# Prompt attention in a hybrid decoder layer: the products with V of a piece as one run behind all of its transposes

## The chip, the cores and the metric

The kernel runs on one core of a Trainium2 chip. A core has a matrix engine, TensorE (PE in the profile; PEld is its weight load, which overlaps the matmuls), and three engines that work on tiles: VectorE (DVE), ScalarE (ACT) and GpSimd (POOL). SyncE (SP) issues this kernel's DMAs, which a set of 16 DMA engines carries out. TensorE reads from the on-chip memory SBUF and writes into the banks of PSUM, from where DVE or ACT fetch the result.

The metric is the time of one execution on the device, in microseconds (us); the median of several runs counts, and less is better. A profiled execution gives the durations of single instructions.

## The reference

One inference step of a decoder layer, for one prompt of 1024 tokens and 8 x 8 sample tokens. Cut to what matters here:

```python
def dilated_group_prompt(q, k, v, window, dilation):      # (128,1), (512,4), (2048,16)
    ...
    s = jnp.einsum('brnqhd,brnkhd->brnhqk', qs, kk) * SCALE
    ...
    s = jnp.where(mask[None, None, :, None], s, NEG_INF)
    o, lse = softmax_attend(s, vv, 'brnhqk,brnkhd->brnhqd')
...
def trunk_layer(x, ...):
    h = rms_norm(x, norm_mix_g)
    proj = h @ w_in
    ...                                  # split into a_val, a_gate, q, k, v
    a = jax.nn.silu(layer_norm(depthwise_conv_valid(a_full, conv_a_w, conv_a_b), ln_a_g, ln_a_b))
    o = attend(q, k, v).reshape(B, S, D_ATTN)
    x = x + jnp.concatenate([a, o], axis=-1) @ w_out
    h = rms_norm(x, norm_ffn_g)
    g = depthwise_conv_valid(g_full, ffn_conv_w, ffn_conv_b)
    x = x + (jax.nn.silu(g) * (h @ w_ffn_up)) @ w_ffn_down
```

There are 12 heads of 64 columns. Each query sees its neighbours at three strides, and the three partial softmaxes are merged, which is the same as one softmax over all the (query, key) pairs with a count for pairs that occur more than once.

## The kernel before

**Stages.** The 1088 tokens (1024 of the prompt, 64 of the samples) lie along the free axis. First come the projections into Q, K and V, one pair of heads (128 columns) after another, six pairs in all; the products of a projection are three for each weight (high and low parts, lines 183 to 185 in `gemm`), accumulated in PSUM tiles `g`. Q, K and V are written to DRAM (`dq`, `dk`, `dv`) and read back per head by `load_head`. Attention of the prompt begins while pair 3 is projected and is spread between the projections of pairs 3 to 5; the rest lies in a stage of its own beside the attention of the samples and the output projection (`out_part`, whose products are also lines 183 to 185 and whose sums into `x` are line 858). The last part of the output projection (lines 960 to 974, products 911 to 914, sums 1061) opens the next stage, and then the feed-forward network follows.

**A piece.** Prompt attention of one head is cut into two pieces of 512 queries (`u` 0 and 1), 24 pieces in all. `scores` (line 650) multiplies Q and K into PSUM `s`, once for the near window ("near", in blocks of neighbouring tokens, Q tile `qw`) and once for the strided neighbours ("far", Q tile `qs`); DVE adds the masks (L654). `exchange` (L628) shares the maxima. Then `weighted` does, for the piece before:

1. the exponentials on ACT (L691), in place, into the weights `y`, queries on the partitions;
2. for each of three (`u` = 0) or four (`u` = 1) **groups** of weights: three or four transposes on TensorE (L718) into one of two PSUM banks `t`; a copy of that bank into an SBUF tile `ph` of the tag "H", by ACT (L724), or for one group by DVE (L722); then the products with V (L735) that use it, V being the stationary operand (64 columns), into the single bank `o`: near ones with `vw` into partitions 0 to 63, far ones with `vf` into 64 to 127;
3. ACT copies one half of `o` out (`ot`, L738) and DVE adds the other (`un`, L739).

`normalise` follows after a pair of heads: `db` (L748), four transposes (L751), the quotient `cat` (L753) and its DMA into `mixed` in DRAM (L755). `load_mixed` (L267 to L270) reads `mixed` back for the output projection and splits it into the parts `mh` and `ml`; L960 to L963 do so for the last part.

**What sets the order.** The program is written in one order; a scheduler with a simulated timeline gives each engine its own order from it, taking among what is ready what has the highest priority, which is by default what was written first. `tc.issue_after(x)` keeps an instruction behind `x` on its engine. Each engine then works through its list strictly in order: an instruction that has to wait holds up everything behind it on that engine. Products with V wait for a place in the list like everything else, so rows of the projections, of `scores` and of other transposes stand between them.

**Buffers.** `KB, VB, QB, YB, HB, UB, PT = 4, 2, 2, 7, 5, 2, 2` in line 51: V has two tiles (`vf`, loaded at L607, and `vw`, loaded at L610 in four DMAs), which is one pair of heads, so the next pair's V can be loaded only after the last product with V of the pair before. Q has two tiles (`qs` by L595 and `qw`, made from it by POOL at L597), one head. H has five tiles, used by `ph`, `ot`, `db` and `cat`; there is one bank `o` and there are two banks `t`. Weight tiles of the output projection (`wr`, L153) have two buffers, and SP issues all DMAs in one list.

Of the kernel before, what the change touches and what calls it, by code (L numbers as in the profile page):

```python
# [24 lines left out]
P = 128  # L25
# [22 lines left out]
NCH = NCACHE // CH  # L48

TB, WB, ZA, GA = 5, 5, 4, 2  # L50
KB, VB, QB, YB, HB, UB, PT = 4, 2, 2, 7, 5, 2, 2
DCOPY = ((2,), (2,))
SBUFS = {"S": (3, 3, 2), "U": (3, 3, 1)}
NS1, PN = 3, 4
HEADS = (0, 5, 8)
# [24 lines left out]
def trunk_kernel(tc, xT, w_in, w_out, w_gate, w_up, w_down, par, kc, vc, sa, sf, pmask, smask,  # L80
                 yT, kT, vT, ca, cas, cf):
    nc = tc.nc
    with (
# [31 lines left out]
        def bank(z, tag, bufs):  # L115
            return zone[z + "ps"].tile([P, 512], F32, tag=tag, name=nm(tag), bufs=bufs)

        def zt(z, tag, bufs, s, w=N, dt=F32):
            return zone[z].tile([P, w], dt, tag=tag, name=nm(s), bufs=bufs)
# [44 lines left out]
        def load_cache(Z, src):  # L164

            t = zt(Z, "C", SBUFS[Z][0], "cr", 4 * CH)
            cached.append(nc.sync.dma_start(t, src).ins)
# [345 lines left out]
        def sample_attention(p, Z, masks):  # L513
            mask, z = masks
            SB, PB = SBUFS[Z][1:]
            _, new, vn = spill[p]
# [166 lines left out]
        def weighted(p, hd, u, sc, den, un):  # L683

            near, far, m = sc
            vf, vw = [v[:, :, hd * 64:hd * 64 + 64] for v in values[p]]
            r0 = slice(hd * 64, hd * 64 + 64)
            r1 = slice(64 - hd * 64, 128 - hd * 64)
            for g, ys in ((0, near), (1, far)):
                for i, y in enumerate(ys):  # L690
                    nc.scalar.activation(y, y, AF.Exp, bias=m[:, 4 * g + i:4 * g + i + 1], scale=-1.0,  # L691
                                         accum_out=den[:, g, 2 * hd + u, i:i + 1])
            po = bank("P", "o", 1)
            pw = po.rearrange("p (c i j) -> p c i j", c=4, j=32)


            near_jobs, far_jobs = [], []
            for kb in range(max(4 * u - 1, 0), 4 * u + 4):
                qs = [i for i in (kb - 4 * u, kb + 1 - 4 * u) if 0 <= i < 4]
                ts = [near[i][:, -P:] if kb == 4 * u + i else near[i][:, :P] for i in qs]  # L700
                near_jobs.append((0, ts, vw[:, kb], pw[:64, :, qs[0]:qs[-1] + 1, :]))
            for c in range(4):
                for k in range(u + 1):
                    far_jobs.append((1, [far[c][:, k * P:k * P + P]], vf[:, 2 * c + k], po[64:, c * P:c * P + P]))

            n, f = near_jobs, far_jobs
            if u == 0:
                group = [[n[0], f[0], f[1]], [n[2], f[2], f[3]], [n[1], n[3]]]
            else:
                group = [[n[1], f[0], f[1]], [n[3], f[2], f[3]], [n[2], f[4], f[5]], [n[0], f[6], n[4], f[7]]]  # L710
            done = [[], []]
            left = [len(n), len(f)]
            for gi, jobs in enumerate(group):
                pt = bank("P", "t", PT)
                o = 0
                for _, ts, _, _ in jobs:
                    for t in ts:
                        nc.tensor.transpose(pt[:, o:o + P], t, ident)  # L718
                        o += P
                th = zt("P", "H", HB, "ph", 512)  # L720
                if gi in DCOPY[u]:
                    nc.vector.tensor_copy(th[:, :o], pt[:, :o])  # L722
                else:
                    nc.scalar.activation(th[:, :o], pt[:, :o], AF.Copy)  # L724
                o = 0
                for x, ts, v, dst in jobs:
                    left[x] -= 1
                    w = P * len(ts)
                    m = th[:, o:o + w]
                    if x == 0:  # L730
                        m = m.rearrange("p (s c j) -> p c s j", c=4, j=32)
                    with ExitStack() as order:
                        for b in (done[x][:1] if x else done[x][:2]):
                            order.enter_context(tc.issue_after(b))
                        done[x].append(nc.tensor.matmul(dst, v, m, start=not done[x], stop=(left[x] == 0)).ins)  # L735
                    o += w
            ot = zt("P", "H", HB, "ot", 512)
            nc.scalar.activation(ot[r0, :], po[r1, :], AF.Copy)  # L738
            nc.vector.tensor_add(un[u][r0, :], po[r0, :], ot[r0, :])  # L739
# [39 lines left out]
        def finish():  # L779
            for b in before:  # L780
                weighted(*b)
                if b[1:3] == (1, 1):
                    normalise(b[0], *b[4:])
            before.clear()
# [47 lines left out]
        first = [0]  # L832
# [121 lines left out]
        n = PARTS[-1]  # L954
# [368 lines left out]
        raws, moving, lows, done = {}, [], [], []  # L1323
# [60 lines left out]
        w, act = [], []  # L1384
# [45 lines left out]
        for k, (g, unit) in enumerate(UNITS):  # L1430
# [16 lines left out]
            for i, product in enumerate(unit):  # L1447
                b, key, outs = product
                for m in range(4):
# [6 lines left out]
                    for r, h in outs:  # L1456
                        x = x2[4 * r + m][:, h * HN:h * HN + HN]
# [176 lines left out]
```

## Time and profile before

| | |
|---|---|
| time, median of 3 runs | 1351.49 us (1349.26 to 1357.11) |
| the profiled execution: its time | 1352.69 us |
| the profiled execution: span of its records | 1350.9 us, mean granted TensorE clock 0.992 |
| TensorE busy in the span | 1313.0 us (97%) |
| DVE, ACT, POOL busy | 945.5 us (70%), 558.2 us (41%), 474.1 us (35%) |
| first and last product with V (L735) | 260.7 us and 568.4 us |

The span is the stretch from the first record to the last; the execution's own time is 1.8 us more. Times in rows count from the start of the span. A row of the timeline has the start, the duration, the engine, the line, the operation, the tile written and the tiles read, the shape, and how many such instructions are put together (x4); in brackets stands how long the engine was idle before it, and what released it. Matmuls overlap in TensorE: of two rows that follow each other without a gap, it is the distance of their starts that counts, not the duration. "PEclk" in a row of a window is the clock that TensorE was granted there, as a share of full speed.

### The profile page before, as it was taken

What the parts mean: (1) busy time and instruction counts of PE and PEld (TensorE: products, weight loads), DVE (VectorE), ACT (ScalarE), POOL (GpSimd) and SP (SyncE); (2) the same over time, 40 slices, a digit from 0 to 9 for tenths busy, and PEclk for the clock granted to TensorE, in tenths of its full rate; (3) what the DMA queues carried; (4) which work ended last, traced back from release to release, by engine and by line L of the source; (5) the groups of instructions that cost most, each with busy time, mean ns of one, the idle gap of its engine ahead of it and who ended that gap; (6) DMA issues with size and microseconds to landing.
All of it is one profiled execution on the core that took longest, in us unless ns stands there. A gap on an engine that the chain in (4) does not pass through costs nothing.

```text
span 1350.9 us, 25872 instructions
## 1 busy us (share of the span) xinstructions
PE 1313.0 (97%) x10275; PEld 1247.8 (92%) x10275; DVE 945.5 (70%) x1789; ACT 558.2 (41%) x1128; POOL 474.1 (35%) x375
## 2 busy tenths in 40 slices
PE   7999999999999999999999999999999999999996
PEld 7999988998977787898999999999999999999996
DVE  6378779556675556768987776677766669967656
ACT  6312111456574466335553333333333335334432
POOL 1321112111111100731475465554655534444710
PEclk9999999999999999999999999999999999999998
DMA  8247684935689786453033322332213296352412
GB/s 287 60 142 278 227 287 173 242 112 144 179 271 268 214 264 206 160 202 110 1 121 106 106 67 86 121 107 104 81 73 121 73 335 233 107 171 98 154 40 95
DMA packets 92762, 210.28 MB, mean 156 GB/s; under 512 B 13792, under 2 KB 42720, under 8 KB 92640
## 3 DMA queue, kind: packets, MB, share of 16 engines
q1 hardware_dynamic: 92640, 208.62, 47.4%
q8 instruction: 81, 1.33, 0.4%
q14 instruction: 41, 0.34, 0.1%
HBM read 152.55 MB, written 56.04 MB: 154 GB/s over the span
## 4 chain that ended last, share of the span: by engine, by line
PE 82%; DVE 8%; DMA 6%; issue 2%; ACT 1%; SPq 1%; DVEq 0%; ACTq 0%
PE g L183 6%; PE g L185 6%; PE g L184 6%; PE py L913 4%; PE py L911 4%; PE py L914 4%; PE g L911 4%; PE g L913 4%; PE g L914 4%; PE o L735 3%; PE pz L911 3%; PE pz L913 3%; PE pz L914 3%; PE px L911 3%; PE px L914 3%; PE px L913 3%
## 5 line engine op out<-in xcount | busy, mean ns | idle before, releaser
L159 POOL TENSOR_TENSOR wl<-wr,wh 128x1024 fp32r<-128x1024 f32 (+1 forms) x36 | 66.8, 1855 | 350.5 <-PE g L185 274.1
L183 PE MATMUL g<-xh,wh 128*128 128x384 f32 (+1 forms) x472 | 157.8, 334 | 0.6 <-DVE qkv L446 0.6
L184 PE MATMUL g<-xl,wh 128*128 128x384 f32 (+1 forms) x472 | 156.6, 332 | 0.0
L185 PE MATMUL g<-xh,wl 128*128 128x384 f32 (+1 forms) x472 | 156.4, 332 | 0.0
L911 PE MATMUL g<-ux,as 128*128 128x272 f32 x504 | 145.1, 288 | 1.0 <-DVE x L1458 0.9
L914 PE MATMUL g<-ux,as 128*128 128x272 f32 x504 | 145.3, 288 | 0.0
L913 PE MATMUL g<-ux,as 128*128 128x272 f32 x504 | 144.7, 287 | 0.0
L1016 POOL TENSOR_TENSOR wb<-wr,wb 128x512 fp32r<-128x512 f32 x84 | 120.9, 1449 | 57.3 <-ACT wb L1015 57.3
L1368 POOL TENSOR_TENSOR as<-ar,as 128x640 fp32r<-128x640 f32 (+1 forms) x56 | 91.3, 1640 | 102.7 <-ACT as L1367 89.9
L1015 ACT ACTIVATE wb<-wr 128x512 fp32r<-128x512 f32 x84 | 52.4, 627 | 154.4 <-DVE wr L1032 94.5
L1016 POOL TENSOR_TENSOR wa<-wr,wa 128x512 fp32r<-128x512 f32 x42 | 65.1, 1553 | 138.4 <-ACT wa L1015 117.3
L691 ACT ACTIVATE y<-y,m 128x128 f32<-128x128 f32 (+1 forms) x192 | 88.4, 463 | 20.0 <-DVE m L679 20.0
L911 PEld LDWEIGHTS g<-ux,as 128*128 128x128 f32 x504 | 95.0, 189 | 1.3 <-ACT as L1367 1.1
L914 PEld LDWEIGHTS g<-ux,as 128*128 128x128 f32 x504 | 94.8, 188 | 0.0
L913 PEld LDWEIGHTS g<-ux,as 128*128 128x128 f32 x504 | 94.7, 188 | 0.0
L654 DVE CUSTOM_DVE_ANT_0 y<-s,pmk 128x128 f32<-128x128 f32 (+1 forms) x192 | 64.1, 378 | 41.7 <-PE s L650 31.7
L1238 DVE SCALAR_TENSOR_TENSOR fc<-gb,prm,fc 128x1104 f32<-128x1104 f32 x44 | 82.5, 1894 | 14.9 <-ACT fc L1236 14.4
L183 PEld LDWEIGHTS g<-xh,wh 128*128 128x128 f32 x472 | 89.0, 189 | 3.1 <-issue 1.8
L185 PEld LDWEIGHTS g<-xh,wl 128*128 128x128 f32 x472 | 89.0, 189 | 2.3 <-issue 2.1
L184 PEld LDWEIGHTS g<-xl,wh 128*128 128x128 f32 x472 | 89.2, 189 | 0.6 <-issue 0.2
L396 DVE SCALAR_TENSOR_TENSOR cacc<-gp,prm,cacc 128x1024 f32<-128x1024 f32 x60 | 86.6, 1443 | 0.0
L157 ACT ACTIVATE wh<-wr 128x1024 fp32r<-128x1024 f32 (+1 forms) x36 | 29.6, 822 | 111.6 <-PE g L185 79.5
(370 smaller groups left out, 4288.7 us busy)
## 6 DMA issues: line engine op xcount, KB each, us to landing
cr<-in_kc SPq DMA_DIRECT2D x24, 768.0 KB, 6.9
cr<-in_vc SPq DMA_DIRECT2D x24, 768.0 KB, 7.3
ux<-ub SPq DMA_DIRECT2D x63, 272.0 KB, 4.3
kk<-dk SPq DMA_DIRECT2D x48, 256.0 KB, 6.1
wr<-in_w_gate SPq DMA_DIRECT2D x22, 512.0 KB, 3.3
wr<-in_w_up SPq DMA_DIRECT2D x22, 512.0 KB, 4.3
wr<-in_w_in SPq DMA_DIRECT2D x20, 512.0 KB, 5.7
ub<-u SPq DMA_DIRECT2D x18, 544.0 KB, 4.4
```

What stands on the lines that cost most here:

```text
L159: lo_eng.tensor_sub(lo, raw, hi.bitcast(F32))
L183: nc.tensor.matmul(ps[c], whi[:, k, :], xh[:, t0:t0 + n], start=(k == 0), stop=False)
L184: nc.tensor.matmul(ps[c], whi[:, k, :], xl[:, t0:t0 + n], start=False, stop=False)
L185: nc.tensor.matmul(ps[c], wlo[:, k, :], xh[:, t0:t0 + n], start=False, stop=(k == nk - 1))
L396: eng.scalar_tensor_tensor(acc[:, :S], gp[:, j:j + S], col(w0 + j), acc[:, :S], op0=ALU.mult, op1=ALU.add)
L691: nc.scalar.activation(y, y, AF.Exp, bias=m[:, 4 * g + i:4 * g + i + 1], scale=-1.0, accum_out=den[:, g, 2 * hd + u, i:i + 1])
L911: nc.tensor.matmul(ps, whi[:, k, :], xh[:, t], start=(start and k == 0), stop=False, skip_group_check=True)
L913: nc.tensor.matmul(ps, whi[:, k, :], xl[:, t], start=False, stop=False, skip_group_check=True)
L914: nc.tensor.matmul(ps, wlo[:, k, :], xh[:, t], start=False, stop=(k == nk - 1), skip_group_check=True)
L1016: nc.gpsimd.tensor_sub(lo, x, hi.bitcast(F32))
L1238: nc.vector.scalar_tensor_tensor(c[:, :W], gb[i][:, t:t + W], col(C_FW + 3 * f + t), c[:, :W], op0=ALU.mult, op1=ALU.add)
L1368: nc.gpsimd.tensor_sub(lo, raw, hi.bitcast(F32))
```

## The change

H gets 8 tiles in the place of 5. `weighted` takes the groups in another order (group 0 last), and for each only transposes and copies; the tiles are kept in `turned`. Then all products with V of the piece follow, each kept directly behind the one before by `tc.issue_after`, the group that was copied last first, and with a priority raised by 4000 places of the written order.

```diff
-KB, VB, QB, YB, HB, UB, PT = 4, 2, 2, 7, 5, 2, 2
+KB, VB, QB, YB, HB, UB, PT = 4, 2, 2, 7, 8, 2, 2
 DCOPY = ((2,), (2,))
+AHEAD = 4000
...
-            done = [[], []]
-            left = [len(n), len(f)]
-            for gi, jobs in enumerate(group):
+            turned = []
+            for gi in (*range(1, len(group)), 0):
+                jobs = group[gi]
                 pt = bank("P", "t", PT)
                 o = 0
                 for _, ts, _, _ in jobs:
...
                     nc.scalar.activation(th[:, :o], pt[:, :o], AF.Copy)
-                o = 0
-                for x, ts, v, dst in jobs:
-                    left[x] -= 1
-                    w = P * len(ts)
-                    m = th[:, o:o + w]
-                    if x == 0:
-                        m = m.rearrange("p (s c j) -> p c s j", c=4, j=32)
-                    with ExitStack() as order:
-                        for b in (done[x][:1] if x else done[x][:2]):
-                            order.enter_context(tc.issue_after(b))
-                        done[x].append(nc.tensor.matmul(dst, v, m, start=not done[x], stop=(left[x] == 0)).ins)
-                    o += w
+                turned.append((jobs, th))
+            done = []
+            left = [len(n), len(f)]
+            with tc.high_priority(offset=AHEAD):
+                for jobs, th in turned[-1:] + turned[:-1]:
+                    o = 0
+                    for x, ts, v, dst in jobs:
+                        w = P * len(ts)
+                        m = th[:, o:o + w]
+                        if x == 0:
+                            m = m.rearrange("p (s c j) -> p c s j", c=4, j=32)
+                        first = left[x] == len((n, f)[x])
+                        left[x] -= 1
+                        with tc.issue_after(done[-1]) if done else nullcontext():
+                            done.append(nc.tensor.matmul(dst, v, m, start=first, stop=(left[x] == 0)).ins)
+                        o += w
```

The number of products, transposes, copies and DMAs is the same. Below, products with V are L735 before and L740 with the change; other lines behind the edit go up by one to five (L183 becomes L184, L718 L719, L724 L725, L738 L743, L650 L651, L269 L270).

**On TensorE, in the first piece** (bank `o_2433`, during a projection, whose products are those into `g`): two of the three groups before, with transposes between them.

```order
L735 MATMUL o_2433<-ph_2439,vw_2321 64x4x64
L735 MATMUL o_2433<-ph_2439,vf_2319 64x128 x2
L718 MATMUL t_2454<-ident,y_2342 128x128
L718 MATMUL t_2454<-ident,y_2350 128x128
L735 MATMUL o_2433<-ph_2449,vw_2321 64x4x64
L735 MATMUL o_2433<-ph_2449,vf_2319 64x128 x2
L718 MATMUL t_2454<-ident,y_2350 128x128
```

The third group stands 24 rows further on, behind products of the projection. With the change, the same place reads:

```order
L184 MATMUL g_3454<-xh_132,wh_3325 128x384
L740 MATMUL o_2433<-ph_2452,vw_2321 64x4x64
L740 MATMUL o_2433<-ph_2452,vf_2319 64x128 x2
L740 MATMUL o_2433<-ph_2439,vw_2321 64x4x64
L740 MATMUL o_2433<-ph_2439,vf_2319 64x128 x2
L740 MATMUL o_2433<-ph_2445,vw_2321 64x4x64
L740 MATMUL o_2433<-ph_2445,vw_2321 64x4x32
L651 MATMUL s_2480<-kk_2374,qw_2372 128x128
```

All products of the piece now stand in one run, from the last group copied to the others, between products of the projection and those of `scores`. Over the whole program there are 67 such runs before and 24, one for each piece, with the change, and TensorE's list changes 234 times before and 160 times with the change between rows that write 128 partitions, 64 and 32.

**On ACT, at the end of the last projection** (the piece whose products go into `o_3843`, pair 2, second head): `ph` are copies of transposed weights, `ot` the copy out of `o`, `y` the exponentials of the next piece, and `mh` the high parts for the output projection. Before:

```order
L738 ACTIVATE ot_3787<-o_3745 64x512
L724 ACTIVATE ph_3849<-t_3844 128x512
L724 ACTIVATE ph_3859<-t_3854 128x512
L691 ACTIVATE y_3808,den_3092<-y_3808,m_3832 128x256 x2
L691 ACTIVATE y_3816,den_3092<-y_3816,m_3832 128x256 x2
L691 ACTIVATE y_3792,den_3092<-y_3792,m_3832 128x256 x2
L691 ACTIVATE y_3800,den_3092<-y_3800,m_3832 128x256 x2
L738 ACTIVATE ot_3872<-o_3843 64x512
L724 ACTIVATE ph_3946<-t_3941 128x512
L724 ACTIVATE ph_3956<-t_3951 128x512
L269 ACTIVATE mh_4619<-mx_4617 128x1088
```

With the change:

```order
L743 ACTIVATE ot_3787<-o_3745 64x512
L270 ACTIVATE mh_4619<-mx_4617 128x1088
L725 ACTIVATE ph_3849<-t_3844 128x512
L270 ACTIVATE mh_4625<-mx_4623 128x1088
L725 ACTIVATE ph_3862<-t_3857 128x512
L270 ACTIVATE mh_4631<-mx_4629 128x1088
L743 ACTIVATE ot_3872<-o_3843 64x512
```

The splits `mh`, which wait for DMAs, stood behind the copies and the `ot` of this piece and now stand between them; the run of products that needs these copies has one small product (a row of `exchange`) between itself and its last transposes on TensorE.

**On TensorE, in the last piece** (`o_5871`, during the output projection): before, its last two groups.

```order
L735 MATMUL o_5871<-ph_5897,vw_5052 64x4x64
L735 MATMUL o_5871<-ph_5897,vf_5050 64x128 x2
L185 MATMUL g_6432<-mh_6282,wl_6416 128x384
L735 MATMUL o_5871<-ph_5907,vw_5052 64x4x32
L735 MATMUL o_5871<-ph_5907,vf_5050 64x128
L735 MATMUL o_5871<-ph_5907,vw_5052 64x4x32
L735 MATMUL o_5871<-ph_5907,vf_5050 64x128
L183 MATMUL g_6443<-mh_6270,wh_6414 128x320
```

With the change:

```order
L186 MATMUL g_6516<-mh_6282,wl_6500 128x384
L740 MATMUL o_5871<-ph_5898,vw_5052 64x4x64
L740 MATMUL o_5871<-ph_5898,vf_5050 64x128 x2
L740 MATMUL o_5871<-ph_5877,vw_5052 64x4x64
L740 MATMUL o_5871<-ph_5877,vf_5050 64x128 x2
L740 MATMUL o_5871<-ph_5884,vw_5052 64x4x64
L740 MATMUL o_5871<-ph_5884,vf_5050 64x128 x2
L740 MATMUL o_5871<-ph_5891,vw_5052 64x4x32
L740 MATMUL o_5871<-ph_5891,vf_5050 64x128
L740 MATMUL o_5871<-ph_5891,vw_5052 64x4x32
L740 MATMUL o_5871<-ph_5891,vf_5050 64x128
L184 MATMUL g_6527<-mh_6270,wh_6498 128x320
```

The run stands later among the rows of the output projection: 119 rows of this stage follow the last product with V before, and 65 with the change. On SP, the last write of `cat` and the reads of `mixed` behind it now come without the last loads of weights between them.

## The prediction

> **What bounds the kernel now.** I read the whole first (shares by engine), then windows over the stretch in which prompt attention runs (255 to 575 us), then TensorE's waits there, and then single places on the timeline. The chain of work that ended last, by engine:
>
> ```profile
> PE 82%; DVE 8%; DMA 6%; issue 2%; ACT 1%; SPq 1%; DVEq 0%; ACTq 0%
> ```
>
> The windows give for each stretch its length, then the busy time of TensorE, of its weight loads, DVE, ACT and POOL with instruction counts, the granted clock, the DMA share and GB/s.
>
> ```profile
> 255.00:300.00 45.00, 45.00 (x320) 40.98 (x318) 25.53 (x99) 25.12 (x79) 6.88 (x4) 1.00 0.56 161
> 300.00:375.00 75.00, 74.47 (x556) 69.02 (x556) 47.61 (x164) 45.95 (x126) 9.93 (x6) 1.00 0.59 164
> 375.00:425.00 50.00, 46.13 (x361) 38.05 (x360) 35.18 (x148) 31.41 (x100) 5.45 (x6) 1.00 0.92 260
> 425.00:500.00 75.00, 74.63 (x666) 60.63 (x666) 40.27 (x173) 41.40 (x130) 8.16 (x8) 0.98 0.79 237
> 500.00:575.00 75.00, 71.52 (x645) 58.04 (x644) 50.29 (x145) 37.70 (x112) 26.26 (x14) 1.00 0.62 197
> 575.00:700.00 125.00, 119.04 (x887) 116.93 (x886) 103.19 (x158) 61.79 (x101) 46.72 (x37) 0.97 0.31 107
> ```
>
> TensorE is busy for 45.00 of 45, 74.47 of 75, 46.13 of 50, 74.63 of 75 and 71.52 of 75 us: attention is bound by TensorE, and what shortens TensorE's list there shortens the kernel. DVE and ACT stand at half to two thirds. The waits of TensorE that matter here between 255 and 575 us (engine, line, releaser: total, times, longest):
>
> ```profile
> PE o L735 <- DMA vw<-dv: 2.0, 1, 2.0
> PE s L628 <- DVE xe L625: 1.4, 2, 1.0
> PE g L183 <- ACT mh L269: 0.8, 1, 0.8
> PE o L735 <- ACT ph L724: 0.7, 1, 0.7
> ```
>
> Copies (L724) hold TensorE up for 0.7 us in all. So the change cannot win by taking waits for copies away; there are none to speak of.
>
> **Term 1: fewer switches on TensorE.** What it can win is the price of going from 128-column rows into products with V (64 columns) and back. During a projection:
>
> ```profile
> 304.76 0.31 PE L183 MATMUL g<-xh,wh 128*128 128x320 f32 x1
> 304.91 0.30 PE L184 MATMUL g<-xl,wh 128*128 128x320 f32 x1
> 305.14 0.43 PE L735 MATMUL o<-ph,vw 128*64 128x256 f32 x1
> ...
> 307.34 0.64 PE L650 MATMUL s<-kk,qw 128*128 128x256 f32 x4
> ...
> 307.91 0.32 PE L735 MATMUL o<-ph,vw 128*64 128x128 f32 x1
> ...
> 308.07 0.27 PE L735 MATMUL o<-ph,vw 128*64 128x128 f32 x1
> ...
> 308.18 0.27 PE L735 MATMUL o<-ph,vw 128*64 128x128 f32 x1
> ...
> 308.29 0.27 PE L735 MATMUL o<-ph,vw 128*64 128x128 f32 x1
> ...
> 308.50 0.75 PE L650 MATMUL s<-kk,qw 128*128 128x256 f32 x4
> ...
> 379.70 0.60 PE L718 MATMUL t<-ident,y 128*128 128x128 f32 x4
> ...
> 381.45 0.66 PE L718 MATMUL t<-ident,y 128*128 128x128 f32 x4
> ```
>
> Starts of 320-column products are 0.15 apart, the first L735 comes 0.23 behind: +0.08 on the way in. Within a run the second L735 comes 0.16 behind the first, later ones 0.11: +0.05. The row behind the last comes 0.21 after it in the place of 0.11: +0.10. And the four L650 behind a run take 0.75, against 0.64 elsewhere: +0.11; four transposes 0.66 against 0.60: +0.06. A run so costs 0.08 + 0.05 + 0.10 + 0.06 to 0.11 = 0.29 to 0.34 us beside its work, say 0.30, or 0.15 for a change of width. The order has 43 runs fewer (67 to 24): 43 x 0.30 = 12.9 us. But a run also goes where a neighbour of another width (L628) had broken the row anyway; counted by changes of width, 74 fewer: 74 x 0.15 = 11.1 us. I take **-11.1**, bounds -13 and -9 (the latter if only the gaps in and out and the refill, 0.23, times 43 = 9.9, are got, and some of it lies beside waits). Nearly all lies where TensorE is dense, so nothing else fills the time won. Transposes, copies, products, transfers and their durations stay: 0.
>
> **Term 2: end of the last projection (390 to 428 us).** Here the trace has idle time of TensorE that the new order moves.
>
> ```profile
> 399.03 1.11 ACT L269 ACTIVATE mh<-mx 128x1088 fp32r<-128x1088 f32 x1 [1.91 <-DMA mx<-mixed]
> ...
> 406.60 0.38 SPq L607 DMA_DIRECT2D vf<-dv  x1
> ...
> 423.49 0.40 PE L735 MATMUL o<-ph,vw 128*64 128x256 f32 x1 [2.01 <-DMA vw<-dv]
> ```
>
> ```profile
> 423.50:428.00 4.50, 4.50 (x24) 3.86 (x25) 0.68 (x1) 1.68 (x3) 0.00 (x0) 0.62 1.03 415
> ```
>
> V of pair 3 is asked for at 406.60 and used at 423.49 after an idle 2.01 us, under a DMA share of 0.92; behind that the clock is 0.62 for 4.5 us, which is 4.5 x 0.38 = 1.7 us of work lost. The load took 16.8 us, of which 14.9 were covered: 10.7 by TensorE's rows between the last product of pair 2 and the first of pair 3 (rows of the order by their distances in the trace), the rest by other waits. With the change these rows come to some 15 us in the same way, 4.3 more than before, which is above the 2.0 that were open, so I let the 2.0 and the 1.7 go. Against that ACT's list has the three `mh` between the copies of one piece: ACT waits for mx (1.91 us in the trace) ahead of copies which TensorE needs almost at once. The price of a copy without cover is shown at the end of the attention:
>
> ```profile
> 522.72 0.60 PE L718 MATMUL t<-ident,y 128*128 128x128 f32 x4
> 523.35 0.60 ACT L724 ACTIVATE ph<-t 128x512 f32<-128x512 f32 x1 [3.67 <-PE t L718]
> ...
> 524.00 0.43 PE L735 MATMUL o<-ph,vw 128*64 128x256 f32 x1 [0.69 <-ACT ph L724]
> ```
>
> That is 0.69 us of idle TensorE with nothing in between. Two such pieces and the mx wait, 2 x 0.69 + 1.91 = 3.3, less the waits of 1.0 (xe) and 0.8 (mh) there now, add 1.5. Sum -3.7 + 1.5 = -2.2, taken as **-2.0**; bounds -4 (the waits now there fall together) and +3 (V is late as before and mx too).
>
> **Term 3: attention beside the output projection (428 to 568 us).** In the order a run of products comes 3 to 6 us of TensorE work behind its last transposes in most pieces, which hides the 1.28 us from the first transpose to the run above; in three pieces only 1.4 to 1.9 us, with ACT shared with `mh` and exponentials. If each pays 0.69, less the 0.7 paid now, that is +1.4. The last head's Q is asked for with 4.3 us of rows ahead of its use, 8.0 before; Q took this long to land:
>
> ```profile
> DMA to landing us min/median/max: 3.4/4.1/11.3
> ```
>
> With its cast on POOL about 5 us: up to +1 in the middle, +7 at the worst. Shorter waits for exponentials (0.5) count against it. I take **+1.5**, bounds -1 and +5. Loads of V for pairs 4 and 5 have 12 and 10.7 us of rows, and landed in 7.1 in the median (its row is quoted with the rivals), so 0.
>
> **Term 4: the end of the attention stage.** The last products with V set `cat`, which goes to DRAM and comes back for the last output part.
>
> ```profile
> 568.36 0.27 PE L735 MATMUL o<-ph,vw 128*64 128x128 f32 x1
> ...
> 576.67 0.46 SPq L755 DMA_DIRECT2D mixed<-cat  x1
> ...
> 582.57 1.33 SPq L960 DMA_DIRECT2D mx<-mixed  x3
> ...
> 588.34 1.96 ACT L962 ACTIVATE mh<-mx 128x544 fp32r<-128x544 f32 x3 [1.97 <-DMA mx<-mixed]
> ...
> 588.54 0.31 PE L185 MATMUL g<-mh,wl 128*128 128x320 f32 x1
> 589.52 0.74 PE L911 MATMUL g<-mh,wh 128*128 128x272 f32 x4 [0.68 <-DVE x L858]
> 591.87 0.59 PE L913 MATMUL g<-ml,wh 128*128 128x272 f32 x1 [1.60 <-DVE ml L963]
> ...
> 593.84 1.11 PE L911 MATMUL g<-mh,wh 128*128 128x272 f32 x4
> ```
>
> 119 rows from 568.6 to 588.85 are 20.3 us, 0.17 each; 65 rows are 11.1 us, 9 us less cover. From the last product to the write are 8.0 us (the transposes of `db` keep their place behind it). The first read doesn't need that write, and no weight load is left between: about 0.4 later, 5.8 to land (582.57 to 588.34), 0.7 to split, ready 14.9 us after the last product, TensorE waits 3.8. The second tile needs the write (2.0, the shortest of L755, to 4.9, since at 581.5 it was over), then 5.8 and 1.4: 17.2 to 20.1, against 14.9 + 2.7 us of products with the first tile: 0 to 2.5 more. In all 3.8 to 6.3, against 0.68 + 1.60 now: +1.5 to +4. I take **+2.5**; bounds -0.7 (read in 3.6, the shortest) and +8 (write 7.6, its median, and a clock drop of 1.7 behind the idle time).
>
> **Sum.** -11.1 - 2.0 + 1.5 + 2.5 = -9.1 from the profiled execution's own 1352.69: 1343.6. That execution lay 1.2 above the median of the runs, so the median should be near 1342.5; I say **1343**. After 590 us TensorE and DVE hand on to each other as before, so what is won by then reaches the end.
>
> **The rivals.** *(a) Given back at the ends.* The switches go, but the thin covers and the way through DRAM take it: Term 2 at 0, Term 3 at +4, Term 4 at +7 give -0.1, 1351; with half of that 1347. For it: DMA share 0.92 and 0.79 in these stretches, and landings of Q up to 11.3. Against: 0.31 at Term 4. *(b) Slower: V comes late.* V can be asked for only after the last product of the pair before, and those products are now at the end of the piece.
>
> ```profile
> DMA to landing us min/median/max: 4.8/7.1/13.3
> ```
>
> If every pair's load takes the 16.8 us from 406.60 to 423.4, against covers of 15, 13.5, 17, 12 and 10.7 us, TensorE waits 1.8 + 3.3 + 0 + 4.8 + 6.1 = 16, 14 more than now; two further clock drops 3.4; with Terms 1, 3, 4 and the 1.5 of Term 2, 1352.7 + 14 + 3.4 - 11.1 + 1.5 + 2.5 + 1.5 - 1.2 = 1363. It decides from about 15 us a load, where waits (8.8) and clock drops eat Term 1. Against: the median of L607 above is 7.1. *(c) All covers hold:* Term 1 at -12, Term 2 at -4, Terms 3 and 4 at +1: 1338. *(d) Longer stretches of transposes lower the clock.* The longest stretch in the order goes from 13 transposes to 16, with another of 15. If the clock fell behind each as at 423.5, 2 x 1.7 = 3.4 us are lost: 1346.4, say 1346. In the trace the clock is 1.00 in the dense windows from 255 on. On this the Trainium skill, "TensorE: Matmul & The Clock Gate", section "Part 4: PE-mode transpose", says that transposes do not count as busy time for the clock gate; by that rule (d) would hold, and the window 300 to 375 us at 1.00 speaks against it, for stretches no longer than those there. The same page, section "Why this matters for your kernels", allows idle gaps up to about 3 us before the clock falls; the row at 423.49 shows it falling after 2.01, and the measurement decides. *That the change does not do what it says* is out: the order has one run per piece.
>
> **How the numbers follow.** Forecast 1343 (1339 to 1346): 0.47. (a) 1347 to 1354: 0.30. (b) 1358 to 1366: 0.10. (c) 1335 to 1339: 0.08. (d) about 1346: 0.05. The half per cent that a measurement can tell from no change is 6.8 us: faster below 1344.7, slower above 1358.3. Faster: (c) and 0.92 of the forecast, 0.08 + 0.43 = 0.51. Slower: (b) and a tail of (a), 0.12. The rest, 0.37, is within. The range leaves out (b) and a part of (c): 1335 to 1356.
>
> **What would show it.** Term 1: 24 runs of L740, TensorE's busy time in attention less by about 11 us. Term 2: no wait of L740 for vw near 423, the clock at 1.00 behind it, waits for `ph` or `mh` ahead of it. Term 3: waits of L740 for L725 below 2 us in all. Term 4: waits of L916 and L918 for mx of 4 to 6 us in the place of 2.3. It is wrong if V's loads are waited for at several pairs, or if TensorE's busy time in attention stays although the runs are fewer.

## The result and the profile after

The changed kernel took 1343.32 us in the median of 6 runs (1337.43 to 1345.38); the kernel before took 1357.35 in 6 runs, three of which are those of the table of its time further up (1349.26 to 1359.47). The ratio is 0.9908, with a 95% interval of 0.9886 to 0.9931: 0.9% faster. Its profiled execution took 1339.82 us, with a span of 1338.0 and a clock of 0.995. The forecast of 1343 and its range of 1335 to 1356 held.

TensorE's line on the first page of the profile after (busy time, share of the span, number of instructions; then its weight loads, DVE, ACT and POOL):

```profile
PE 1297.1 (97%) x10275; PEld 1245.7 (93%) x10275; DVE 937.9 (70%) x1789; ACT 559.8 (42%) x1128; POOL 477.0 (36%) x375
```

TensorE has the same 10275 instructions and is busy 15.9 us less. The windows over the same clock times as before, of the kernel after:

```profile
255.00:300.00 45.00, 45.00 (x330) 43.12 (x329) 26.31 (x105) 26.41 (x82) 6.86 (x4) 1.00 0.61 184
300.00:375.00 75.00, 75.00 (x578) 72.13 (x577) 45.81 (x165) 48.20 (x135) 9.53 (x6) 1.00 0.63 173
375.00:425.00 50.00, 46.35 (x368) 39.68 (x367) 35.59 (x142) 31.29 (x89) 6.47 (x7) 1.00 0.88 275
425.00:500.00 75.00, 74.17 (x741) 61.30 (x740) 43.18 (x176) 43.35 (x133) 7.14 (x7) 1.00 0.87 260
500.00:575.00 75.00, 69.54 (x612) 62.48 (x612) 50.33 (x157) 37.85 (x116) 27.99 (x16) 1.00 0.60 169
```

The stage is as dense as it was, but there is more in the same time: in the 375 to 500 us TensorE starts 1109 instructions, 1027 before. What counts is a window that holds the same work in both: from one product of the projection ahead of all attention, at 250.22 and 253.71 us, to the first row of the norm behind the last output part (L205, now L206), at 611.79 and 601.74. The first row is of before, the second of after.

```profile
250.22:611.79 361.57, 350.46 (x2800) 304.79 (x2799) 226.47 (x773) 198.90 (x575) 68.51 (x47) 0.99 0.68 205
```

```profile
253.71:601.74 348.03, 334.18 (x2799) 302.08 (x2799) 225.07 (x773) 200.83 (x575) 69.29 (x48) 1.00 0.72 213
```

361.57 against 348.03 us: the stretch is **13.5 us shorter**, and TensorE is busy 16.3 less in it. Outside it the pair of traces gives back 3.5 us ahead of the stretch (253.71 - 250.22) and gains 2.9 behind it, where the change has no hand in the work: 13.5 - 3.5 + 2.9 is the 12.9 between the spans. In the thirteen traces of this case the stretch begins anywhere from 250.2 to 257.8 us, though TensorE's order up to there is the same. In the five traces with the change's order this start differs by 6.6 us and the stretch itself by 1.8; that is the reason why I compare this stretch from here on.

One run of the kernel after, in the first piece:

```profile
270.12 0.34 PE L184 MATMUL g<-xh,wh 128*128 128x384 f32 x1
270.39 0.43 PE L740 MATMUL o<-ph,vw 128*64 128x256 f32 x1
270.39 0.43 PE L740 MATMUL o<-ph,vf 128*64 128x128 f32 x2
270.65 0.38 PE L740 MATMUL o<-ph,vw 128*64 128x256 f32 x1
...
270.87 0.38 PE L740 MATMUL o<-ph,vw 128*64 128x256 f32 x1
...
271.30 0.81 PE L740 MATMUL o<-ph,vw 128*64 128x256 f32 x4
272.05 0.73 PE L651 MATMUL s<-kk,qw 128*128 128x128 f32 x4
```

In: 0.27 behind a product whose successors come 0.17 to 0.18 apart. The first pair takes 0.26, the others 0.21 to 0.22. This price is now paid 24 times and not 67. Added up over all runs from the starts in the traces (the way in, the run itself, the way out to the next row and the delay of the row behind, idle time left out), the runs cost 62.2 us before and 47.2 after, for the same products: 15.0 us, or 0.35 for each of the 43 runs that are gone.

### The profile page after: what moved, and what is told of

The parts are those of the page before. It is cut to its first block, busy times and chain, and to the rows that moved or that the text cites. A ratio compares the mean times of both kernels' runs of the same rounds, so it can differ in the third digit from the quotient of the medians.

```text
span 1338.0 us, 25862 instructions
## 1 busy us (share of the span) xinstructions
PE 1297.1 (97%) x10275; PEld 1245.7 (93%) x10275; DVE 937.9 (70%) x1789; ACT 559.8 (42%) x1128; POOL 477.0 (36%) x375
## 4 chain that ended last, share of the span: by engine, by line
PE 56%; DVE 3%; issue 1%; ACT 0%; DMA 0%; DVEq 0%; ACTq 0%
PE g L918 5%; PE g L919 5%; PE g L916 5%; PE py L918 5%; PE py L916 4%; PE py L919 4%; PE px L916 3%; PE pz L918 3%; PE px L919 3%; PE pz L919 3%; PE pz L916 3%; PE px L918 3%; PE g L1490 1%; PE g L1491 1%; PE g L1492 1%; DVE sq L1073 1%
## 5 line engine op out<-in xcount | busy, mean ns | idle before, releaser
L184 PE MATMUL g<-xh,wh 128*128 128x384 f32 (+1 forms) x472 | 158.3, 335 | 0.6 <-DVE qkv L447 0.6
L1243 DVE SCALAR_TENSOR_TENSOR fc<-gb,prm,fc 128x1104 f32<-128x1104 f32 x44 | 83.4, 1914 | 14.8 <-ACT fc L1241 14.5
L1021 POOL TENSOR_TENSOR wa<-wr,wa 128x512 fp32r<-128x512 f32 x42 | 57.6, 1375 | 97.5 <-ACT wa L1020 73.6
L184 PEld LDWEIGHTS g<-xh,wh 128*128 128x128 f32 x472 | 89.4, 189 | 3.0 <-issue 1.6
L1463 DVE TENSOR_TENSOR x<-g,x 128x544 f32<-128x544 f32 x76 | 52.5, 717 | 32.9 <-PE g L919 32.9
```

The lines of the kernel that those rows point to most:

```text
L184: nc.tensor.matmul(ps[c], whi[:, k, :], xh[:, t0:t0 + n], start=(k == 0), stop=False)
L1021: nc.gpsimd.tensor_sub(lo, x, hi.bitcast(F32))
L1243: nc.vector.scalar_tensor_tensor(c[:, :W], gb[i][:, t:t + W], col(C_FW + 3 * f + t), c[:, :W], op0=ALU.mult, op1=ALU.add)
```

## The experiments

The table has, for the kernels that differ in runs or buffers, the runs of products with V in its order, the runs' cost added up as above, TensorE's idle time in the stretch (gaps over 0.06 us), the stretch's length, and the ratio to the kernel before with its interval.

| kernel | runs | cost of the runs, us | idle, us | stretch, us | ratio |
|---|---|---|---|---|---|
| before | 67 | 62.2 | 11.0 | 361.6 | 1 |
| after | 24 | 47.2 | 13.8 | 348.0 | 0.9908 (0.9886 to 0.9931) |
| a_again | 24 | 48.5 | 10.4 | 347.1 | 0.9927 (0.9905 to 0.9949) |
| no_ahead | 24 | 47.2 | 14.5 | 348.6 | 0.9923 (0.9899 to 0.9948) |
| h5 | 24 | 48.8 | 13.5 | 348.9 | 0.9935 (0.9910 to 0.9959) |
| after_v4 | 24 | 47.2 | 11.6 | 347.5 | 0.9910 (0.9885 to 0.9935) |
| h8_only | 67 | 63.1 | 11.9 | 361.6 | 0.9997 (0.9976 to 1.0018) |
| before_v4 | 69 | 64.0 | 7.6 | 358.7 | 1.0016 (0.9992 to 1.0039) |
| two_runs | 43 | 53.1 | 16.2 | 358.2 | 1.0006 (0.9981 to 1.0031) |

The table is the answer in short: the kernels with 24 runs in it have a stretch of 347 to 349 us and are 0.65 to 0.92% faster, those with more have 358 to 362 and aren't. These five share one order on TensorE, so they are one point, measured five times. Two other orders with 24 runs, narrow and balanced below, have 361.1 and 352.2 us: the number of runs alone does not set the time. The 48.5 and 48.8 in the column of costs are the same runs with one of them, in the trace, at a lower clock.

**The change once more (a_again).**

> The changed kernel once more, beside the next three on the same chip. Theory (the gain is the switches of TensorE between products of 128 and of 64 columns): 24 runs of products with V, some 7 us spent on entering and leaving them against 18.7 before, ratio 0.988 to 0.993. Rival (the gain is a wait that happened to fall away, above all the 2.0 us for V with its clock drop): then the ratio lies at 0.995 or above once the wait for V is absent from the runs of before too.

0.9927. The interval overlaps the first one, and the trace has 48.5 us for the runs, 13.7 less than before where 11.7 were expected, and no wait for V. The condition of the rival, that before's runs also lack the wait for V, is tested below (before_v4).

**The parts of the change that are not the loop (h8_only, h5, no_ahead).**

```diff
-KB, VB, QB, YB, HB, UB, PT = 4, 2, 2, 7, 5, 2, 2      # h8_only, on the kernel before
+KB, VB, QB, YB, HB, UB, PT = 4, 2, 2, 7, 8, 2, 2
```

> The kernel before with 8 tiles H in the place of 5, and nothing else. Theory (switches): the order keeps 67 runs, entering and leaving them costs 18 to 19 us as before, ratio 0.997 to 1.003. Rival (buffers: more tiles free the copies and so TensorE): ratio 0.990 to 0.994, as with the whole change.

0.9997, and a stretch as long as before:

```profile
253.22:614.82 361.60, 349.51 (x2799) 302.91 (x2799) 227.52 (x773) 198.87 (x575) 68.17 (x47) 1.00 0.69 205
```

The order of all engines is the same as before, row for row. The tiles alone do nothing.

```diff
-KB, VB, QB, YB, HB, UB, PT = 4, 2, 2, 7, 8, 2, 2      # h5, on the changed kernel
+KB, VB, QB, YB, HB, UB, PT = 4, 2, 2, 7, 5, 2, 2
```

> The changed kernel with 5 tiles H, as before the change; the order on every engine is the same row for row, and only which tile is waited for differs. Theory (switches alone): as the change, ratio 0.990 to 0.995. Rival (the 8 tiles are needed, since a piece keeps four copies until its run): ACT and DVE wait for tiles H, TensorE for the copies, 5 us and more of new waits, ratio 0.996 or above.

0.9935 with a stretch of 348.9 us: the loop doesn't need the 8 tiles either. Five are enough for four copies and an `ot`.

```diff
-            with tc.high_priority(offset=AHEAD):       # no_ahead, on the changed kernel
+            with nullcontext():
```

> The changed kernel without the raised priority: the order still has 24 runs, each at the place that the written order gives it. Theory (switches): the same 12 us are won, and only waits differ, ratio 0.988 to 0.995. Rival (the raised priority is what wins, since it frees the bank o and V early): ratio 0.997 or above, with waits of TensorE for V or for weights of the next stage of 5 us and more.

0.9923. Here the experiment was emptier than I took it for: without the raised priority the order on all five engines is the change's own, row for row, and so it is with an offset of 300, 1000 or 12000, whose programs were built but not timed. So this is a third measurement of one program, and the raised priority has no effect. What the change does is done by the loop alone.

**Half of the runs (two_runs).** Two groups are transposed, copied and multiplied, then the others:

```diff
-            for gi in (*range(1, len(group)), 0):
-                jobs = group[gi]
...
-            with tc.high_priority(offset=AHEAD):
-                for jobs, th in turned[-1:] + turned[:-1]:
+            for part in (range(2), range(2, len(group))):
+                turned = []
+                for gi in part:
+                    jobs = group[gi]
...
+                with tc.high_priority(offset=AHEAD):
+                    for jobs, th in turned[::-1]:
```

> The changed kernel, but each piece in two halves: two groups are transposed and copied and then multiplied, then the rest; the order has 43 runs. Theory (switches, 0.34 us each): 19 runs more than with the change cost 6.5 us, ratio 0.994 to 0.998, and entering and leaving costs about 13 us in the trace. Rival (it is not the number of runs, but that a run comes late behind its copies or the ends of the stage): within 2 us of the change, ratio 0.989 to 0.993.

The runs cost 53.1 us, 5.9 more than with 24 runs (19 x 0.31): that step is as expected. But the ratio is 1.0006, and the stretch is 10.2 us longer than with the change, not 6.5:

```profile
251.00:609.22 358.22, 341.93 (x2800) 303.84 (x2799) 223.90 (x773) 198.37 (x574) 67.15 (x47) 1.00 0.68 206
```

The rest is 2.4 us of idle time more (among it a wait for V of 1.4 us that neither the change nor its repetitions have) and some 2 us that equal products took longer (the clock is at 0.50 for 3.41 us from 589.9). So in this trace the price of the runs with 43 of them lay where it should. The time does not bear it out: 1.0006 is outside the 0.994 to 0.998 expected, so half of the runs did not give half of the gain. The stretch of the trace is 3.4 us shorter than before, which would be 0.9975 and lies just below the interval (0.9981 to 1.0031); but the profiled execution, 1347.75 us, is the fastest of the twelve, whose median is 1357.03. What takes the gain in the others is not shown.

**The price of a width alone (breaks, narrow).** 60 products of 32 columns with zeros, between the groups of a run:

```diff
-                for jobs, th in turned[-1:] + turned[:-1]:
+                for gi, (jobs, th) in enumerate(turned[-1:] + turned[:-1]):
+                    if gi:
+                        with tc.issue_after(done[-1]):
+                            done.append(nc.tensor.matmul(po[:, :32], zeros[:, :128], ident[:, :32], start=False,
+                                                         stop=False, skip_group_check=True).ins)
                     o = 0
```

with `po[:64, :32], zeros[:, :64]` in narrow.

> The changed kernel with 60 small products more: between the groups of each run one product of 32 columns with a stationary tile of 128 columns of zeros is added to the bank o, which leaves the sums as they are. Each breaks a run into two. Theory (going from 64 columns of width to 128 and back costs 0.34 us): 60 x 0.34 = 20 us, and 60 x 0.06 = 4 us for the products themselves, 24 us more than the changed kernel, ratio 1.006 to 1.012 against the kernel before. Rival (the 0.34 us are no matter of the width, but of the start of a run, its waits or its first weights): less than 8 us more, ratio 0.992 to 0.998, the same as the kernel with narrow zeros.

> The same 60 products, with a stationary tile of 64 columns of zeros, into the lower half of the bank o, so that no run is broken. Theory (width): only the work, 60 x 0.06 to 0.1 = 4 to 6 us more than the changed kernel, ratio 0.994 to 0.998, and 15 to 20 us less than with 128 columns. Rival: no difference between the two.

breaks took 1383.3 us, ratio 1.0212 (1.0186 to 1.0238); narrow 1357.99, ratio 1.0019 (0.9992 to 1.0046): 25.3 us apart, or 0.42 for each of 60. In the traces the runs cost 25.8 us more in breaks than in narrow, 0.43 each, of which some 3 us are a lower clock in a few runs of breaks. First breaks, then narrow, from the first group of a run to the second:

```profile
267.56 0.43 PE L746 MATMUL o<-ph,vw 128*64 128x256 f32 x1
...
268.14 0.30 PEld L735 LDWEIGHTS o<-ident,zeros 128*128 128x128 f32 x2 [0.17 <-issue]
268.15 0.41 PE L735 MATMUL o<-ident,zeros 128*128 128x32 f32 x2
...
268.49 0.43 PE L746 MATMUL o<-ph,vw 128*64 128x256 f32 x1
```

```profile
271.50 0.43 PE L746 MATMUL o<-ph,vw 128*64 128x256 f32 x1
...
271.76 0.14 PEld L735 LDWEIGHTS o<-ident,zeros 128*64 128x64 f32 x1
...
271.98 0.19 PE L735 MATMUL o<-ident,zeros 128*64 128x32 f32 x1
...
272.06 0.41 PE L746 MATMUL o<-ph,vw 128*64 128x256 f32 x1
```

From group to group it is 0.93 us in breaks, 0.56 in narrow, and 0.48 in the change (270.39 to 270.87). Width decides, as expected: at this place products just as many and just as short cost 0.08 in the run's own width and 0.45 in the other, and over whole runs at full clock 0.11 and 0.49 (a run with two of them takes 1.89 and 2.65 us, one with three 2.23 and 3.37; the change's take 1.66 and 1.90).

Where the price comes from stands in the rows of the weight loads (PEld), which I had not looked at. The load of the narrow zeros starts 0.22 us ahead of their product (271.76, 271.98) and so lies beside the products in front of it; that of the wide ones starts with it (268.14, 268.15), after 0.17 us in which the loads stood still and waited for nothing that the profile shows ("issue"). In the stretch of before the load starts within 0.01 us of its product at 172 of the 184 rows that follow one of another width, and a median of 0.11 us ahead of it at the other rows. By these records a change of width is a place where the weight load is not overlapped.

The sizes were off. The 25 us are more than the 15 to 20 expected, in part because each of the two passes of a wide zero product takes 0.13 us by itself (row starts), so the switch proper is about 0.45 - 0.27 = 0.2 us here; the 0.35 of a run that is gone holds the delay of the 128-column rows behind it as well. Against the change with 5 tiles H in the same session (h5, 1345.21 us), breaks is 38 us slower and not 24, and narrow 13 and not 4 to 6. Their runs at full clock are 29.5 and 6.7 us longer. Part of the rest goes with the clock in these traces: within the stretch it is at 0.50 for 9 times 3.41 us in breaks, 3 times in narrow and once in h5. What else is in it is not shown.

**V one pair ahead (before_v4, after_v4).** 4 tiles V in the place of 2, on the kernel before and on the changed one.

```diff
-KB, VB, QB, YB, HB, UB, PT = 4, 2, 2, 7, 5, 2, 2      # before_v4; with HB = 8 in after_v4
+KB, VB, QB, YB, HB, UB, PT = 4, 4, 2, 7, 5, 2, 2
```

> The kernel before with 4 tiles V in the place of 2, so that the next pair's V is loaded while the pair before is still multiplied; its order has 69 runs. It prices the wait for V that is there before the change and not with it (2.0 us, and 1.7 us of lower clock behind it). Theory (the gain of the change is the switches): the wait for V is gone from the trace and 2 to 4 us with it, ratio 0.996 to 1.000, far from the change. Rival (the wait for V that fell away is a large part of the gain): ratio 0.994 or below.

> The changed kernel with 4 tiles V; the order on TensorE is the change's, row for row, and only the loads of V are asked for earlier. The trace of the change shows no wait for V, so theory: no difference, ratio 0.990 to 0.994. Rival (V is in the way of other loads where it is now asked for, in the stretch with a DMA share of 1.0): 2 us and more better, ratio 0.990 or below, or worse by as much when the earlier loads are in the way of Q and K.

Without its wait for V the kernel before stays where it is: 1.0016. Its stretch:

```profile
254.46:613.11 358.65, 350.87 (x2799) 303.58 (x2799) 226.99 (x773) 199.26 (x575) 68.10 (x47) 1.00 0.68 206
```

That is 2.9 us shorter than before, with TensorE as busy (350.87 against 350.46): what the wait for V is worth in the trace, at most a fifth of what the change is worth, and in the times it is worth nothing. The rival of a_again falls with it: with four tiles V on both sides the ratio is 1342.79 / 1354.86 = 0.991. after_v4 is at 0.9910, within the spread of the change's own measurements; V is not what the changed kernel waits for.

**A try at a faster one (balanced, balanced_v4).** Near products fill the lower half of `o` and far ones the upper; they run side by side, 7 blocks against 4 in pieces with `u` = 0. One near block moves up:

```diff
+            up = [n[3]] if u == 0 else []
...
-            left = [len(n), len(f)]
+            left = [len(n) - len(up), len(f) + len(up)]
+            sizes_ = list(left)
...
-                        first = left[x] == len((n, f)[x])
+                        if any(job is b for b in up):
+                            x, dst = 1, pw[64:, :, 3:4, :]
+                        first = left[x] == sizes_[x]
```

> The changed kernel, with one near product of the pieces with u = 0 (the one of 128 columns) put into the upper half of the bank o, where the far products are added up; both halves are added in the end, so the result is the same sum. In the trace of the changed kernel near and far products run side by side, and a piece with u = 0 has 7 blocks of 128 near ones and 4 far ones. Theory (the longer half sets the length of a run): 6 and 5 blocks, a block of 0.22 us less in each of 12 runs, 2.6 us, ratio 0.988 to 0.992. Rival (the products start in the order in which they stand and don't make use of it): run length and time as with the change.

> The changed kernel with one near product of the pieces with u = 0 in the upper half of the bank, 4 tiles V and 5 tiles H: a try at a kernel that is faster than both. If the 2.6 us that the runs are shorter are not eaten by waits as in the same kernel with two tiles V (3.4 us for a load of the sample's cache there), ratio 0.987 to 0.991; if they are, 0.992 to 0.996.

The runs do get shorter. The first one of balanced, its first product and the row behind its last:

```profile
267.31 0.43 PE L745 MATMUL o<-ph,vw 128*64 128x256 f32 x1
...
268.75 0.44 PE L651 MATMUL s<-kk,qw 128*128 128x128 f32 x2
```

1.44 us, against 1.66 in the change (270.39 to 272.05): the 0.22 that a block takes. But the stretch is 352.2 and 353.8 us, longer than the change's, with TensorE's clock down behind waits in several places. One of them in balanced, 4.5 us at 0.62:

```profile
441.90:446.40 4.50, 4.48 (x20) 4.50 (x21) 1.25 (x10) 3.52 (x14) 1.04 (x1) 0.62 1.01 320
```

The ratios, 0.9944 (0.9920 to 0.9967) and 0.9909 (0.9884 to 0.9935), are not better than those of the change. The arithmetic of the runs was right; whether the waits come with the new order or with these executions isn't settled by one trace each.

## Why the prediction was right, step by step

**Term 1, the switches: right, a little small.** Predicted -11.1, bounds -13 to -9. The runs cost 15.0 us less; outside them TensorE changes width more often than before (62 times, 50 before, not counting runs), which costs 1.8 more: **-13.2**. I counted 74 changes of width at 0.15; counted by runs, 43 at the 0.30 of the rows, it would have been 12.9. The price I read was 0.30 a run, the traces give 0.35. The trace of two_runs (0.31 a run) and breaks against narrow bear the mechanism out. What the prediction had as gaps in and out is, by the weight-load rows above, the load that is not overlapped.

**Term 2, end of the last projection: right in this pair of traces, in part by luck.** Predicted -2.0. The wait for V and the clock drop behind it are gone. V is asked for at 411.56 and used at 429.77, 18.2 us later and without a wait; and it landed sooner. From the timeline and the window of after, and the row of landings of V's first load:

```profile
411.56 0.38 SPq L608 DMA_DIRECT2D vf<-dv  x1
```

```profile
423.50:428.00 4.50, 4.50 (x33) 4.47 (x31) 2.44 (x15) 4.50 (x19) 0.85 (x1) 1.00 1.04 300
```

```profile
DMA to landing us min/median/max: 4.8/6.0/9.1
```

The longest landing is 9.1 us, 13.3 before. These are landings of one DMA; the whole load of pair 3, from its first row to the last of the four `vw`, took 7.5 us, 16.6 before. None of the five traces with the change's order on TensorE has a wait for V in attention; before and h8_only, with one order, wait 2.0 and 3.8 us. The price, too, came where the order of ACT showed it, `mh` and `ph` in turn:

```profile
389.39 0.62 PE L184 MATMUL g<-mh,wh 128*128 128x384 f32 x2 [1.03 <-ACT mh L270]
...
391.50 0.43 PE L740 MATMUL o<-ph,vw 128*64 128x256 f32 x1 [0.83 <-ACT ph L725]
```

Waits from 375 to 428 us are 3.65 us (3.77 before), and 1.7 of clock is won: -1.8. In waits the new order so gives only 0.1. The 1.7 is not safe: before and h8_only both have a drop behind the wait for V, but a_again and h5, with the change's order, have one of 3.41 us at 0.50 behind these two waits for ACT (the row of a_again is in the last section).

**Term 3, beside the output projection: right in size by luck, wrong in place.** Predicted +1.5; TensorE's waits from 428 to 568 us grew from 3.9 to 6.3, **+2.4**. But the covers of the copies held, with no wait of a run for its copy there. The largest waits between 255 and 590 us after the change:

```profile
PE g L184 <- DVE x L863: 2.2, 1, 2.2
PE t L719 <- ACT y L692: 1.5, 2, 1.4
PE g L918 <- DVE ml L968: 1.5, 1, 1.5
PE g L184 <- ACT mh L270: 1.0, 1, 1.0
PE s L651 <- DMA qs<-dq: 1.0, 2, 0.6
PE o L740 <- ACT ph L725: 0.8, 1, 0.8
```

They are for DVE's sums of the output projection (2.2), which I had not named, and for the exponentials (1.4), whose waits I had expected to get shorter. The 2.2 doesn't come in a_again, so it is not fixed by the order: over the five traces with this order the waits from 428 to 568 us are 3.2 to 7.7 us.

**Term 4, the end of the stage: wrong in size.** Predicted +2.5, bounds -0.7 to +8; measured **0**: 0.78 + 1.47 us of waits at the first products of the last part, 0.68 + 1.60 before. The chain in the trace after (issues on SP, then ACT, then TensorE):

```profile
575.86 0.34 SPq L760 DMA_DIRECT2D mixed<-cat  x1
576.25 0.42 SPq L965 DMA_DIRECT2D mx<-mixed  x1
...
577.96 1.27 SPq L965 DMA_DIRECT2D mx<-mixed  x3
579.23 0.66 ACT L967 ACTIVATE mh<-mx 128x544 fp32r<-128x544 f32 x1 [4.40 <-DMA mx<-mixed]
...
579.94 0.77 PE L916 MATMUL g<-mh,wh 128*128 128x272 f32 x4 [0.78 <-ACT mh L967]
...
582.18 0.39 PE L918 MATMUL g<-ml,wh 128*128 128x272 f32 x1 [1.47 <-DVE ml L968]
```

The 8.0 us up to the write are there (567.8 to 575.86), and the write was waited for some 2 us (the reads behind it go out at 577.96). The step that failed is "5.8 to land": the first read landed in 3.0 us (576.25 to 579.23). I had taken 5.8 from the wrong row, the first of three reads that go out together at 582.57. The first read of before goes out alone at 581.55, right behind a load of weights, and landed in 3.6, which the prediction used only for its lower bound. From SP's rows of before, and the landings of its four reads:

```profile
581.08 0.38 SPq L968 DMA_DIRECT2D wr<-in_w_out  x1
581.55 0.46 SPq L960 DMA_DIRECT2D mx<-mixed  x1
582.05 0.42 SPq L1153 DMA_DIRECT2D sft<-in_sf  x1
```

```profile
DMA to landing us min/median/max: 3.6/5.8/6.1
```

The second wait is for DVE's split, and as long as before.

**The sum.** -13.2 - 1.8 + 2.4 + 0 = -12.6, and 1.4 us more by a clock drop at 590 us in the trace of before (0.86 from 587.5 to 600) that is missing after: 14.0, where the stretch shows 13.5. Predicted -9.1. Of the 14.0, the 1.7 and the 1.4 are clock drops, and the clock is not what the change wins in the median: over the timed executions of the later sessions its mean is 0.991 before and 0.989 to 0.990 with the change's order. Without these drops some 11 us are left, and the times say the same: by the first ratio it is 12.5 us (9.4 to 15.5), over the five measurements with the change's order on TensorE (0.9908 to 0.9935) some 10 to 11. Terms 1 and 4 were too pessimistic by 2.1 and 2.5 us, Term 3 too optimistic by 0.9, and Term 2, without the clock, by 1.9.

That the median came out at 1343.32, beside the forecast of 1343, is in part luck. The forecast took 8.5 us off a median of 1351.49; in the six runs the kernel before took 1357.35, and 14.0 less with the change. In the later sessions the medians are 1354.8 to 1355.2 before and 1342.8 to 1345.3 with the change's order.

**The rivals.** (a), given back at the ends, fell with Term 4. (b), V late, fell: the whole loads of V (one `vf` and four `vw`) took 7.5 to 11.8 us, and its point of decision was 15. The median of 7.1 that the prediction set against it is of one DMA, not of a whole load. (c), 1338, was the best case of all, and the profiled execution, 1339.82, came near it; the median didn't. (d) has nothing for it: in the stretch with the long rows of transposes the clock is 1.00 in each of the five windows above. The rule of the Trainium skill, "TensorE: Matmul & The Clock Gate", section "Part 4: PE-mode transpose", that transposes do not count as busy time, had no effect on the clock that shows here.

## What to carry to other kernels

On an engine that is always busy, price the neighbours of an instruction, not only the instruction: the same 504 products cost 15 us less because they stand together in 24 runs and not in 67. Price such a change by the distances of starts at the seams in the trace of before, and count the seams in both orders; the first sits in a few rows of the timeline, the second in the two lists of instructions. Take the latency of a transfer from a row that goes out as it will, alone or in a group, and count no clock drop of a single trace as won. When an edit has several parts, compare their orders first: here two of three parts changed no row.

## What was unexpected in the hardware

Idle time of like length sometimes brings the clock down and sometimes not. It fell to 0.62 for 4.5 us behind a wait of 2.01 us (before, at 423.5), and to 0.62 behind one of 1.8 us (balanced, at 441.9); behind one of 2.20 us in the kernel after it stayed at 1.00:

```profile
540.95:545.45 4.50, 4.50 (x29) 4.47 (x30) 4.47 (x20) 2.54 (x10) 4.50 (x3) 1.00 0.50 161
```

The length of the wait alone doesn't decide it. The clock's records in the traces show what does. Between 12 and 1320 us of all thirteen traces a clock below full comes in whole multiples of 3.41 us at 0.50 (the 0.62 is the mean over 4.5 us), and within one execution these begin on one grid with steps of 3.41 us: in the trace of before at 424.60 and 591.85, which is 49 steps. The wait of 2.01 us lies within one step of that grid; the one of 2.20 us is cut by the edge of a step at 539.7 into about 0.95 and 1.25. The windows are steps of the grid, of before, of after, and of a_again, where two waits behind each other fall into one step:

```profile
421.18:424.60 3.42, 1.41 (x17) 1.11 (x16) 1.29 (x6) 0.00 (x0) 0.82 (x1) 1.00 1.01 312
424.60:428.01 3.41, 3.41 (x12) 2.88 (x11) 0.68 (x1) 1.68 (x3) 0.00 (x0) 0.50 1.03 416
```

```profile
536.29:539.70 3.41, 2.46 (x20) 2.19 (x18) 3.41 (x2) 1.69 (x7) 3.41 (x2) 1.00 0.73 200
539.71:543.12 3.41, 2.17 (x14) 2.18 (x15) 3.41 (x13) 2.94 (x13) 3.41 (x3) 1.00 0.77 278
543.12:546.53 3.41, 3.41 (x31) 3.21 (x31) 3.38 (x11) 0.37 (x1) 3.41 (x3) 1.00 0.26 78
```

```profile
392.59:396.00 3.41, 1.80 (x16) 1.59 (x18) 3.41 (x10) 3.38 (x5) 0.00 (x0) 1.00 1.02 419
396.00:399.41 3.41, 3.41 (x17) 2.52 (x14) 2.56 (x6) 1.44 (x3) 0.00 (x0) 0.50 1.06 291
```

From 100 to 1320 us in the thirteen traces, each of the 32 steps at full clock in which TensorE is idle for more than 1.9 us is followed by one at 0.50; of those with 1.4 to 1.9 us idle it is 12 of 30, of those with less 4 of 4528. The grid lies elsewhere in each execution, so whether a wait of some 2 us costs 1.7 us more is luck. So 1.7 us a drop belongs to the range of a forecast, and not to its sum.
